# A hybrid decoder step on one core: the first four projection jobs taken on the centred input, the norm applied to their results

## The chip, the cores and the metric

The kernel runs on one core of one Trainium2 chip. The metric is the device time of one execution in microseconds. TensorE (PE, with its weight loads PEld) does matrix products and transposes, VectorE (DVE), ScalarE (ACT) and GpSimd (POOL) work element by element, SyncE (SP) issues most transfers. "Granted clock" is the share of the full TensorE clock that the profile shows as granted.

## The reference

One layer of a decoder with two head groups is applied to 272 prompt tokens (16 learned meta tokens and 256 of the prompt) and 32 sample tokens (8 x 4), 304 in all, width 2048. It starts with a LayerNorm, and what follows reads only its output:

```python
xp = _layernorm(concatenate([meta, x_prompt], axis=1), ln0_g, ln0_b)
xs = _layernorm(x_sample, ln0_g, ln0_b)
# in the layer
proj = x @ w_in                       # 2048 -> 7168
q, zf, v, g, gate_b, gate_c, xin = split(proj, ...)
zf = zf + b_f
...
mix = concatenate([o_a, y_b], axis=-1) @ w_o
h   = _layernorm(ALPHA * x + mix, ln1_g, ln1_b)
ff  = (silu(h @ w_gate) * (h @ w_up)) @ w_down
out = _layernorm(ALPHA * h + ff, ln2_g, ln2_b)
```

`_layernorm` is (x - mean) * rsqrt(var + eps) * gain + bias, per token. From q, zf, v and g a gated recurrence over the tokens is made for 8 heads (the scan), from the last three a gated convolution. All weights are float32 and are read once.

## The kernel before

**Projections as jobs.** Activations lie transposed in SBUF: channels on the partitions in 16 blocks of 128, tokens (304, or the 288 without meta tokens) along the free axis. Each weight matrix is read in pieces of 4 channel blocks by 256 columns, 512 KB. A piece is loaded by SP's queue into one of five raw buffers (`load_ahead`, L112; it runs five pieces ahead) and split in two (`split_next`, L128): "hi" is ScalarE's copy in the format fp32r, "lo" is VectorE's difference raw - hi. Up to five pieces lie split. The input is split in the same way into xh and xl. `run_job` (L169) makes 256 output columns: for each of 16 channel blocks and each of two PSUM banks, three products hi·xh, hi·xl and lo·xh (L184 to L186), 96 products a job. The first four jobs belong to the first pair of heads: zb (the forget gate), vb, qb and gb; then follow the other pairs, the convolutions, the output projection and the feed-forward part.

**What sets the order.** The instructions are put in order ahead of the run by a scheduler. It may move an instruction past others on its engine, except those that go through an `InOrder` wrapper (`vec`, `act`, `pe`), which stay in the order of the program; those show up under the wrapper's line, L56 (its shift through the change is to L58). The opening is written through these wrappers, the splits of the first eight pieces among them. TensorE, with 98% of the span, takes its instructions strictly in the order that results. Beside the jobs run "lanes" of small steps (`side`, `tick`, L146 to L161): after each channel block of a job every lane may do its next step. The lane "evac" copies the results of a job from PSUM after `LAG` = 4 ticks (`evac`), the lane "scan" does the recurrence.

**The opening** (L320 to L462). SP loads the meta tokens, the first half of the first 112 prompt rows, the short third token tile, the other halves, the second tile in two halves, then gain and bias of the first norm as 32 rows (`prow0`) and the weights. POOL makes the identity matrix and loads the other small parameters (`prows`, `crows`, `brow`). Tiles xt0 and xt1 hold 128 tokens each, xt2 the last 48. VectorE gets mean and variance of xt0 and xt1 with `bn_stats` on quarters, ScalarE the sums and squares of xt2; `rstd` (L350) makes 1/sqrt and refines it by one Newton step. `norm_rows` (L371) normalises the tiles in place, a quarter at a time, on VectorE and ScalarE. TensorE then transposes each block k (`turn`, L382, three transposes into one bank), and `settle` (L391) applies gain and bias (VectorE, tile xf), copies to xh (ScalarE) and subtracts for xl (every fourth on VectorE, the others on POOL). `turn` and `settle` run `LEAD` = 4 blocks ahead of the first job, zb, which is run inside the opening (L451). After it POOL makes the masks and constants for the scan (`make_constants`), TensorE transposes the parameter rows (L454 to L461), and `lower_bounds` (L275) works out the floor of the forget gate, for which ScalarE loads another function table (L273). The first piece is split block by block, its low part on POOL (L136).

## Time and profile before

| | |
|---|---|
| median of 3 runs | 1411.84 us (1411.36 to 1413.54) |
| profiled execution | 1411.89 us |
| its span | 1410.2 us |
| mean granted clock | 0.995 |
| busy PE | 1382.0 us, 98% |
| busy DVE | 831.2 us, 59% |
| busy ACT | 587.9 us, 42% |
| busy POOL | 115.6 us, 8% |
| moved by DMA | 231.12 MB, mean 164 GB/s |

The span counts from the first to the last event of the profiled execution; the rest of its time, 1.7 us, lies around it. The busy share is a mean over the whole kernel. The change touches the first part alone, so the stretches of the opening and the waits inside it say more than the shares. In rows of the timeline the first number is the start in us, the second the length; in square brackets stands how long the engine had been idle and what it waited for. In rows of groups "x16" is the count, then come total, mean (or least, median, greatest) times.

### The profile page before, as it was taken

The page shows a single profiled execution, that of the slowest core. Times are in us where ns is not written, and L with a number is a line of the kernel's source. Part 1 is how long each engine was busy: PE and PEld are TensorE (multiplying, and loading weights), DVE is VectorE, ACT ScalarE, POOL GpSimd, SP SyncE. Part 2 cuts the span into 40 slices and gives each one's busy share as a digit, 9 for nine tenths or more (in the row PEclk, how much of TensorE's full clock was granted, in tenths as well). Part 3 has the DMA queues.
Part 4 walks back from the last instruction along what each step waited for, and adds up shares of the span by engine and source line. Part 5 has one row for each costly group of instructions (what it writes and reads, how often), then busy time and mean ns, then how long its engine had stood idle before and what let it go on. Part 6 is the DMA issues. An engine that isn't in the chain of part 4 may idle for free.

```text
span 1410.2 us, 24922 instructions
## 1 busy us (share of the span) xinstructions
PE 1382.0 (98%) x10311; PEld 1365.6 (97%) x10311; DVE 831.2 (59%) x1342; ACT 587.9 (42%) x823; POOL 115.6 (8%) x174
## 2 busy tenths in 40 slices
PE   5999999999999999999999999999999999999996
PEld 4999999999999999999999999999999999999995
DVE  6756676876676888966444444444444444465444
ACT  5645544555443444434333333333333333343330
POOL 5201121111000332000000000000000000020000
PEclk9999999999999999999999999999999999999998
DMA  6655655555545554555555555555555555565541
GB/s 188 208 162 162 181 167 168 173 150 169 170 148 165 161 161 151 177 165 165 165 165 165 167 152 167 166 167 181 165 165 165 165 165 165 165 196 165 157 128 68
DMA packets 223858, 231.12 MB, mean 164 GB/s; under 512 B 7756, under 2 KB 219576, under 8 KB 223546
## 3 DMA queue, kind: packets, MB, share of 16 engines
q1 hardware_dynamic: 220240, 218.54, 50.9%
q0 software_dynamic: 3312, 10.72, 2.7%
q8 instruction: 81, 1.33, 0.4%
q10 hardware_dynamic: 192, 0.26, 0.1%
q14 instruction: 33, 0.27, 0.1%
HBM read 222.34 MB, written 7.15 MB: 163 GB/s over the span
## 4 chain that ended last, share of the span: by engine, by line
PE 98%; DVE 1%; POOL 1%; issue 0%; DVEq 0%; ACT 0%; POOLq 0%
PE u L184 7%; PE g L184 7%; PE wd L186 7%; PE g L185 7%; PE u L185 7%; PE wd L185 7%; PE g L186 7%; PE u L186 7%; PE wd L184 7%; PE wo L186 2%; PE wo L185 2%; PE wo L184 2%; PE zb L184 2%; PE zb L185 1%; PE zb L186 1%; PE vb L184 1%
## 5 line engine op out<-in xcount | busy, mean ns | idle before, releaser
L75 DVE TENSOR_TENSOR lo<-raw,hi 128x1024 fp32r<-128x1024 f32 (+1 forms) x408 | 501.7, 1231 | 476.5 <-ACT hi L74 476.0
L74 ACT CAST hi<-raw 128x1024 fp32r<-128x1024 f32 (+1 forms) x408 | 421.3, 1033 | 635.5 <-PE u L185 162.6
L185 PE MATMUL wd<-al,hi 128*128 128x288 f32 x704 | 207.9, 295 | 0.0
L184 PE MATMUL wd<-ah,hi 128*128 128x288 f32 x704 | 207.8, 295 | 0.0
L186 PE MATMUL wd<-ah,lo 128*128 128x288 f32 x704 | 207.8, 295 | 0.0
L184 PE MATMUL g<-ygh,hi 128*128 128x288 f32 (+1 forms) x452 | 134.0, 296 | 0.0
L185 PE MATMUL u<-ygl,hi 128*128 128x288 f32 (+1 forms) x452 | 133.9, 296 | 0.0
L185 PE MATMUL g<-ygl,hi 128*128 128x288 f32 (+1 forms) x452 | 133.9, 296 | 0.0
L184 PE MATMUL u<-ygh,hi 128*128 128x288 f32 (+1 forms) x452 | 133.8, 296 | 0.0
L186 PE MATMUL g<-ygh,lo 128*128 128x288 f32 (+1 forms) x452 | 133.6, 296 | 0.0
L186 PE MATMUL u<-ygh,lo 128*128 128x288 f32 (+1 forms) x452 | 133.6, 296 | 0.0
L185 PEld LDWEIGHTS wd<-al,hi 128*128 128x128 f32 x704 | 132.3, 188 | 0.0
L186 PEld LDWEIGHTS wd<-ah,lo 128*128 128x128 f32 x704 | 132.2, 188 | 0.0
L184 PEld LDWEIGHTS wd<-ah,hi 128*128 128x128 f32 x704 | 132.1, 188 | 0.1
L186 PEld LDWEIGHTS u<-ygh,lo 128*128 128x128 f32 x452 | 85.4, 189 | 0.0
L184 PEld LDWEIGHTS g<-ygh,hi 128*128 128x128 f32 x452 | 85.3, 189 | 0.1
L186 PEld LDWEIGHTS g<-ygh,lo 128*128 128x128 f32 x452 | 85.3, 189 | 0.0
L185 PEld LDWEIGHTS g<-ygl,hi 128*128 128x128 f32 x452 | 85.3, 189 | 0.1
L185 PEld LDWEIGHTS u<-ygl,hi 128*128 128x128 f32 x452 | 85.3, 189 | 0.0
L184 PEld LDWEIGHTS u<-ygh,hi 128*128 128x128 f32 x452 | 85.3, 189 | 0.0
L186 PE MATMUL wo<-mh,lo 128*128 128x288 f32 x256 | 75.9, 296 | 0.0
L185 PE MATMUL wo<-ml,hi 128*128 128x288 f32 x256 | 75.6, 295 | 0.0
(391 smaller groups left out, 3132.3 us busy)
## 6 DMA issues: line engine op xcount, KB each, us to landing
raw<-in_w_in SPq DMA_DIRECT2D x112, 512.0 KB, 3.7
raw<-in_w_gate SPq DMA_DIRECT2D x88, 512.0 KB, 3.6
raw<-in_w_up SPq DMA_DIRECT2D x88, 512.0 KB, 3.6
raw<-in_w_down SPq DMA_DIRECT2D x79, 512.0 KB, 3.6
raw<-in_w_o SPq DMA_DIRECT2D x32, 512.0 KB, 3.6
s<-in_state_hgrn POOLq DMA_DIRECT2D x8, 512.0 KB, 5.5
out<-sn POOLq DMA_DIRECT2D x8, 512.0 KB, 4.4
raw<-in_w_down SPq DMA_DIRECT2D x15, 256.0 KB, 2.8
```

Source lines behind the costliest of these rows:

```text
L74: a.copy(out=hi, in_=src)
L75: v.tensor_tensor(out=lo, in0=src, in1=hi.bitcast(F32), op=ALU.subtract)
L184: nc.tensor.matmul(o, hi[:, i % kb, cs], xh, start=(i == 0), stop=False)
L185: nc.tensor.matmul(o, hi[:, i % kb, cs], xl, start=False, stop=False)
L186: nc.tensor.matmul(o, lo[:, i % kb, cs], xh, start=False, stop=(i == nk - 1))
```

## The change

The first four jobs no longer read the normalised input. They read the tokens with gain applied and roughly centred, and the norm is applied to their results. This is possible because the norm only scales and shifts each token: with c any number per token, x_norm·W = r·[(x - c)·g·W] + r·(c - mean)·[g·W] + [b·W]. The last two brackets are columns that don't depend on the token.

- c (`xcen`) is the token's mean over the first channel block alone, made by one product with a matrix of 1/128 (`ones_h`). `settle` subtracts it in VectorE from the transposed block (xc), ScalarE multiplies with the gain (mh), VectorE makes the low part in one step (ml). The gain g and the bias b stand as two more columns behind the tokens in mh and ml, so that products of these jobs are 306 or 290 wide and yield g·W and b·W.
- Mean and variance are got during the first job: `bn_stats` on quarters after the first two blocks of each four, the sums of xt2 (`row_sums`) on ScalarE at blocks 13 and 15. Behind the job's last product, `rstd` gives r and -mean·r per token, two groups of three products (rb) spread them over the partitions, and xr = r and xnm = c·r - mean·r are made.
- `evac_raw` takes the place of `evac` for the first four jobs: copy of the two columns, multiply by xr, add xnm times the first column, and then the job's own step with the second column as bias.
- The real xh and xl, which later jobs need, are made in a new lane "norm" (`normed_input`) during jobs two to four, 48 steps. After the fourth job `open_scan` ends that lane, gives the memory to the scan, and calls `make_constants`, which stood behind the first job.
- Loads: the tokens come in quarters of 512 channels. ScalarE's queue takes the first quarter of the three short pieces, SP the quarters of xt0 and xt1 with whole weight pieces between. POOL's queue takes the rows of gain and bias (they were SP's last before the weights), then the rest of the short pieces and the other rows.
- The low part of the first piece goes from POOL to VectorE, `LEAD` from 4 to 3, and two products (`WARM`) without use for the result open TensorE's work. sfin has one buffer instead of two.

The core of the diff:

```diff
-LEAD = 4
+LEAD = 3
+NXC = 4
+WARM = 2
...
-                nc.gpsimd.tensor_tensor(out=lo[:, k], in0=raw[:, k], in1=hi[:, k].bitcast(F32), op=ALU.subtract)
+                vec.tensor_tensor(out=lo[:, k], in0=raw[:, k], in1=hi[:, k].bitcast(F32), op=ALU.subtract)
...
+        for dst, src in small:
+            act.dma_start(out=dst[:, :XC], in_=src[:, :XC])
+        tc.keep_in_program_order(nc.scalar.preload_act_table_set("sqrt_and_others"))
+        for c in range(NXC):
+            cs = slice(c * XC, (c + 1) * XC)
+            nc.sync.dma_start(out=xts[0][NMETA:, cs], in_=xin[: P - NMETA, cs])
+            nc.sync.dma_start(out=xts[1][:, cs], in_=xin[P - NMETA : 2 * P - NMETA, cs])
+            load_to(c + 1)
         load_ahead(0)
+        pool.memset(ones_h, 1.0 / P)
+        load_rows(pool, prow0, 0, ("ln0_g", "ln0_b"))
+        for dst, src in small:
+            pool.dma_start(out=dst[:, XC:], in_=src[:, XC:])
...
+        for _ in range(WARM):
+            nc.tensor.matmul(warm, ident, ident.unsqueeze(1).broadcast_to([P, 4, P]), start=True, stop=True)
...
         def settle(k):
             if k < NB:
-                b = xT.pop(k)
-                xf = x0w.tile([P, T], F32, tag="xf", name="xf", bufs=4)
-                vec.tensor_scalar(out=xf, in0=b[:, :T], scalar1=pcol("ln0_g", k), scalar2=pcol("ln0_b", k), op0=ALU.mult, op1=ALU.add)
-                act.copy(out=xh[:, k], in_=xf)
-                xfs[k] = xf
+                vec.tensor_tensor(out=xc[:, k], in0=xT.pop(k)[:, :T], in1=xcen, op=ALU.subtract)
+                act.activation(out=mixh[:, k, :T], in_=xc[:, k], func=AF.Copy, scale=pcol("ln0_g", k))
             if k:
-                eng = vec if k % 4 == 1 else nc.gpsimd
-                eng.tensor_tensor(out=xl[:, k - 1], in0=xfs.pop(k - 1), in1=xh[:, k - 1].bitcast(F32), op=ALU.subtract)
+                vec.scalar_tensor_tensor(out=mixl[:, k - 1, :T], in0=xc[:, k - 1], scalar=pcol("ln0_g", k - 1),
+                                         in1=mixh[:, k - 1, :T].bitcast(F32), op0=ALU.mult, op1=ALU.subtract)
...
+        turn(0)
+        x0c = x0p.tile([P, T], F32, name="x0c")
+        vec.tensor_copy(out=x0c, in_=xT[0][:, :T])
         pb = bank("pb", "main")
-        nc.tensor.transpose(pb[:, :NP0], prow0, ident[:NP0, :NP0])
+        nc.tensor.transpose(pb[:, T : T + NP0], prow0, ident[:NP0, :NP0])
+        nc.tensor.matmul(pb[:, :T], ones_h, x0c, start=True, stop=True)
+        act.copy(out=xcen, in_=pb[:, :T])
...
         def first_rhs(k):
-            c = k // 2 + 2
-            if k % 2 == 0 and c < 4:
-                norm_rows(0, c, act)
-                norm_rows(1, c, vec)
-                norm_rows(2, c, vec)
             if k + LEAD < NB:
-                turn(k + LEAD, (0, 1, 2))
+                turn(k + LEAD)
             if k + LEAD <= NB:
                 settle(k + LEAD)
-            return xh[:, k], xl[:, k]
-
-        first_job = run_job(first_rhs, T, "zb")
-        make_constants()
+            c, i = divmod(k, 4)
+            if i < 2:
+                vec.bn_stats(out=bns[i][:, c], in_=xts[i][:, c * XC : (c + 1) * XC])
+            if k in (13, 15):
+                next(sums)
+            return mixh[:, k], mixl[:, k]
+
+        first_job = run_job(first_rhs, T + 2, "zb")
+        for i in range(2):
+            vec.bn_aggr(out=sts[i][0], in_=bns[i])
+        for _ in zip_longest(*(rstd(i) for i in range(3))):
+            pass
+        rb = [bank("rb") for _ in range(2)]
+        for q in range(2):
+            for i in range(3):
+                nc.tensor.matmul(rb[q][:, i * P : i * P + rows[i]], rn[:, i, q : q + 1].broadcast_to([P, P]), ident[:, : rows[i]],
+                                 start=True, stop=True)
+        act.copy(out=xr, in_=rb[0][:, :T])
+        vec.tensor_mul(out=xnm, in0=xcen, in1=xr)
+        vec.tensor_tensor(out=xnm, in0=xnm, in1=rb[1][:, :T], op=ALU.add)
...
+    def evac_raw(n, banks, out, tag, fn):
+        yield LAG
+        for j in range(2):
+            t = ep_.tile([P, n], F32, tag=tag, name=tag, bufs=4)
+            u = ep_.tile([P, 2], F32, tag="u", name="u", bufs=2)
+            nc.vector.tensor_copy(out=u, in_=banks[j][:, n : n + 2])
+            nc.vector.tensor_mul(out=t, in0=banks[j][:, :n], in1=xr[:, T - n :])
+            nc.vector.scalar_tensor_tensor(out=t, in0=xnm[:, T - n :], scalar=u[:, 0:1], in1=t, op0=ALU.mult, op1=ALU.add)
+            fn(j, t, t, u[:, 1:2])
```

In the orders below a row holds line, operation, output<-inputs and the output's shape; numbers behind names tell tiles apart.

The start of TensorE's order, before: the rows of gain and bias are transposed first (pb from prow0), then four blocks of xt0, of xt1 and of xt2.

```order
L423 MATMUL pb_193<-ident_72,prow0_67 128x32
L387 MATMUL xT_208<-ident_72,xt0_103 128x128
L387 MATMUL xT_210<-ident_72,xt0_103 128x128
L387 MATMUL xT_212<-ident_72,xt0_103 128x128
L387 MATMUL xT_214<-ident_72,xt0_103 128x128
L387 MATMUL xT_208<-ident_72,xt1_104 128x128
```

The same place now: L397 is `turn`, L426 the transpose of those rows, L427 the product that gives c.

```order
L369 MATMUL warm_156<-ident_69 128x512 x2
L397 MATMUL xT_170<-ident_69,xt0_109 128x128
L397 MATMUL xT_170<-ident_69,xt1_110 128x128
L397 MATMUL xT_170<-ident_69,xt2_111 128x128
L426 MATMUL pb_176<-ident_69,prow0_106 128x32
L397 MATMUL xT_181<-ident_69,xt0_109 128x128
L397 MATMUL xT_181<-ident_69,xt1_110 128x128
L397 MATMUL xT_181<-ident_69,xt2_111 128x128
L397 MATMUL xT_185<-ident_69,xt0_109 128x128
L397 MATMUL xT_185<-ident_69,xt1_110 128x128
L397 MATMUL xT_185<-ident_69,xt2_111 128x128
L427 MATMUL pb_176<-x0c_174,ones_h_79 128x304
```

The transpose of prow0 has moved behind the first block, and the product for c stands behind it and six further transposes.

VectorE's order inside the first job, before: gain and bias (xf), low parts (xl, every fourth), tokens normalised in place, and the low part of a weight piece (lo).

```order
L56 TENSOR_SCALAR xf_254<-xT_250,pvec_69 128x304
L56 TENSOR_SCALAR xf_268<-xT_264,pvec_69 128x304
L56 TENSOR_TENSOR xl_96<-xf_254,xh_95 128x304
L56 TENSOR_SCALAR xt1_104<-xt1_104,mv1_142,r1_144 128x512
L56 TENSOR_SCALAR xt2_105<-xt2_105,mv2_147,r2_149 48x512
L56 TENSOR_SCALAR xf_285<-xT_281,pvec_69 128x304
L56 TENSOR_SCALAR xf_299<-xT_295,pvec_69 128x304
L56 TENSOR_TENSOR lo_312<-raw_120,hi_311 128x1024
```

And now, about the same blocks: xnm still holds c here, and each subtraction (xc) is followed by a low part (ml).

```order
L58 TENSOR_TENSOR xc_102<-xT_229,xnm_93 128x304
L58 SCALAR_TENSOR_TENSOR ml_98<-xc_102,pvec_67,mh_97 128x304
L58 BN_STATS bn1_160<-xt1_110 128x6
L58 TENSOR_TENSOR xc_102<-xT_243,xnm_93 128x304
L58 SCALAR_TENSOR_TENSOR ml_98<-xc_102,pvec_67,mh_97 128x304
L58 TENSOR_TENSOR xc_102<-xT_256,xnm_93 128x304
L58 SCALAR_TENSOR_TENSOR ml_98<-xc_102,pvec_67,mh_97 128x304
L58 TENSOR_TENSOR lo_272<-raw_126,hi_271 128x1024
```

Every block now has a low part on VectorE, the statistics stand between them, and the low part of a weight piece stands directly behind that of a block.

ScalarE's order at the end of the first job, before: the last two xh, two weight casts, the function table and the exponentials of `lower_bounds` (ee, lse), and an activation of the scan (w1).

```order
L56 CAST xh_95<-xf_409 128x304
L56 CAST xh_95<-xf_423 128x304
L56 CAST hi_435<-raw_124 128x1024
L56 CAST hi_439<-raw_309 128x1024
L273 ACT_TABLE_LOAD
L285 ACTIVATE ee_523<-dd_520 128x16
L507 ACTIVATE w1_998<-z_605 128x304
L289 ACTIVATE lse_527<-es_525 128x8
L56 CAST hi_561<-raw_371 128x1024
L56 CAST hi_565<-raw_433 128x1024
```

And now: the sums of xt2 (junk, s2), three square roots (t0 to t2), the copy of r (xr), the table and the exponentials.

```order
L58 ACTIVATE mh_97<-xc_102,pvec_67 128x304
L58 ACTIVATE junk_415,s2_416<-xt2_111 48x2048
L58 ACTIVATE junk_415,s2_416<-xt2_111,s2_416 48x2048
L58 ACTIVATE t0_163<-mv0_161,epsb_146 128x1
L58 ACTIVATE t1_166<-mv1_164,epsb_146 128x1
L58 ACTIVATE t2_169<-mv2_167,epsb_146 48x1
L58 COPY xr_92<-rb_463 128x304
L274 ACT_TABLE_LOAD
L286 ACTIVATE ee_485<-dd_482 128x16
L290 ACTIVATE lse_489<-es_487 128x8
L58 CAST hi_512<-raw_329 128x1024
L58 CAST hi_516<-raw_389 128x1024
```

The two casts of the second job's last pieces (hi_512 and hi_516 here) still stand behind the table and the exponentials, but the chain of the statistics is now ahead of those.

More of the change, by code (lines that the diff above doesn't have):

```diff
@@ L112, in load_ahead, with load_to @@
     def load_ahead(i):
[L113 removed]
+        load_to(i + AHEAD_DMA)
+    def load_to(n):
+        while state["dma"] < min(len(pieces), n):
             p = state["dma"]
@@ L380, in hybrid_step, with turn @@
-        xT = {}
-        def turn(k, tiles):
-            if k not in xT:
-                xT[k] = bank("xT")
-            for i in tiles:
-                n = rows[i]
-                nc.tensor.transpose(xT[k][:, i * P : i * P + n], xts[i][:n, k * P : (k + 1) * P], ident[:n, :n])
-        xfs = {}
+        xT = {}
+        def turn(k):
+            xT[k] = bank("xT")
+            for i in range(3):
+                nc.tensor.transpose(xT[k][:, i * P : (i + 1) * P], xts[i][:, k * P : (k + 1) * P], ident)
@@ new lines, in hybrid_step @@
+        turn(0)
+        x0c = x0p.tile([P, T], F32, name="x0c")
+        vec.tensor_copy(out=x0c, in_=xT[0][:, :T])
+        pb = bank("pb", "main")
+        nc.tensor.transpose(pb[:, T : T + NP0], prow0, ident[:NP0, :NP0])
+        nc.tensor.matmul(pb[:, :T], ones_h, x0c, start=True, stop=True)
+        act.copy(out=xcen, in_=pb[:, :T])
+        vec.tensor_copy(out=pvec[:, :NP0], in_=pb[:, T : T + NP0])
+        for k in range(1, LEAD):
+            turn(k)
+        for k in range(LEAD):
+            settle(k)
```

197 lines of the change are left out of this document (97 added, 100 removed).

## The prediction

> **What bounds the kernel now.** Time per stage comes first, then TensorE's waits, then its timeline through the opening. Columns of the first fence: stretch in us, its length, busy time with instruction count of PE, PEld, DVE, ACT, POOL, granted clock, DMA share, GB/s.
>
> ```profile
> 0.00:20.00 20.00, 3.57 (x14) 2.29 (x14) 9.72 (x36) 9.93 (x16) 12.24 (x53) 1.00 0.92 262
> 20.00:40.80 20.80, 20.77 (x109) 17.03 (x108) 16.30 (x26) 11.30 (x21) 9.95 (x13) 1.00 0.32 96
> 58.74:84.00 25.26, 25.26 (x194) 25.26 (x193) 14.91 (x25) 12.05 (x19) 3.55 (x1) 1.00 0.59 180
> ```
>
> TensorE does nearly nothing for 20 us and is then always busy. So a change in the opening is worth exactly what it moves a fixed point of TensorE's order; I take the first product of the third job (qb), behind which nothing on TensorE changes but two columns. The waits (total, times, longest, in us) and the timeline (start, length) say where it stands:
>
> ```profile
> PE pb L423 <- DMA prow<-in_ln_b: 13.2, 1, 13.2
> PE mb L56 <- DVE mq L56: 2.3, 1, 2.3
> PE xT L387 <- DVE xt L56: 1.9, 1, 1.9
> ...
> PE ca L962 <- DVE yc L1012: 0.4, 1, 0.4
> ...
> 20.15 0.85 PE L184 MATMUL zb<-xh,hi 128*128 128x304 f32 x2
> 24.11 0.46 PE L184 MATMUL zb<-xh,hi 128*128 128x304 f32 x1
> 24.36 0.46 PE L185 MATMUL zb<-xl,hi 128*128 128x304 f32 x1
> 28.58 0.30 PE L186 MATMUL zb<-xh,lo 128*128 128x304 f32 x1
> 28.72 0.30 PE L184 MATMUL zb<-xh,hi 128*128 128x304 f32 x1
> 58.74 0.29 PE L184 MATMUL qb<-xh,hi 128*128 128x288 f32 x1
> ```
>
> The first product starts at 20.15; until about 28.1 products step by 0.25 us, later by 0.14 (the clock rows show 1.00 throughout). qb starts at 58.74. The profiled run took 1411.89 us, its span 1410.2; the median of the runs is 1411.84, so no correction lies between them. A measurement can tell about 0.2%, 2.8 us: "same" is 1409.1 to 1414.7.
>
> **The change: the start.** The norm's chain before the first product goes. In its place TensorE's order has the ln0 rows' transpose ahead of six token transposes and of the mean's product, so all of them wait for two row transfers, which the change moves from SP to POOL's queue. Prices:
>
> ```profile
> 2.12 0.32 POOL masks.py:199 TENSOR_SCALAR_AFFINE_SELECT ident<-ident 128x128 f32<-128x128 f32 x1
> 2.36 0.54 POOL L211 DMA_DIRECT2D prows<-in_lb_param  x1
> ...
> prows<-in_lb_param POOLq DMA_DIRECT2D x1, 8.0 KB, 5.8
> prows<-in_gnorm_g POOLq DMA_DIRECT2D x1, 4.0 KB, 6.8
> ...
> out<-sfin POOLq DMA_DIRECT2D x8, 64.0 KB, 3.5
> ...
> 14.48 1.12 PE L387 MATMUL xT<-ident,xt 128*128 128x128 f32 x4 [0.95 <-ACT xt L56]
> 123.16 0.65 PE L666 MATMUL nb<-w,ones_h 128*128 128x288 f32 x2
> 17.33 0.17 DVE L56 COPY pvec<-pb 128x32 f32<-128x32 f32 x1
> L749 ACT COPY vT<-vb 128x304 f32<-128x304 f32 x2 | 0.8, 416 | 0.4 <-PE vb L186 0.4
> ```
>
> The second row transfer follows the identity's select and one memset, so it is issued at about 2.5. Such transfers land 5.8 to 6.8 us later when the queues are full, 3.5 when they are not: 6.0 to 9.3, and I take 8.3, since 2.5 MB lies in SP's queue then as now. Then 0.28 for the transpose, 1.5 for six more, 1.2 for the mean's product (0.65 at full step, up to double at the slow one), 0.42 and 0.17 for the two copies: VectorE subtracts the first block's mean at 11.9. The second token quarter sits behind four weight pieces in SP's order, 3.1 MB; the transfers of before had moved that much at 13.4, and the first product can't start before 14.8 (casts and gain columns, 2.9 us): no cost.
>
> ```profile
> GB/s 0 145 308 173 180 292 382 262 349 348 348 349 342 20 15 285 50 57 293 0 0 5 43 317 1 0 193 156 0 55 145 324 352 281 339 350 350 344 348 338
> ```
>
> (Slices of 1.5 us.)
>
> **The change: the first job.** VectorE now has, until it subtracts block 15: 16 subtractions from PSUM, 14 low halves, 6 row statistics, 4 quarter pieces and 5 whole pieces of weights. Rows of the same forms:
>
> ```profile
> 97.68 0.98 DVE L746 TENSOR_SCALAR z<-zb,pvec 128x304 f32<-128x304 f32 x2 [0.72 <-PE zb L186]
> L830 DVE SCALAR_TENSOR_TENSOR ygl<-yc,pvec,ygh x16: 505/1058/1068, 466.6 to 548.2; 128x288 fp32r<-128x288 f32 x16
> 12.68 2.47 DVE L56 BATCH_NORM_STATS2 bn<-xt 128x6 f32<-128x512 f32 x4
> 60.29 0.42 DVE L556 TENSOR_TENSOR w<-b 128x256 f32<-128x256 f32 x1
> 60.63 1.22 DVE L75 TENSOR_TENSOR lo<-raw,hi 128x1024 fp32r<-128x1024 f32 x1
> 61.76 0.18 DVE L557 TENSOR_TENSOR w<-b 128x32 f32<-128x32 f32 x1
> 31.61 1.32 DVE L56 TENSOR_TENSOR lo<-raw,hi 128x1024 fp32r<-128x1024 f32 x1 [1.46 <-ACT hi L56]
> L829 ACT ACTIVATE ygh<-yc,pvec x16: 520/536/541, 466.0 to 546.0; 128x288 fp32r<-128x288 f32 x16
> L56 ACT CAST hi<-raw 128x1024 fp32r<-128x1024 f32 x7 | 7.1, 1041 | 0.0
> ```
>
> From start to start (an instruction begins about 0.08 before its forerunner's printed end): 16 x 0.45 = 7.2, 14 x 0.45 = 6.3 (the fast end of 505 to 1058: the slow ones stand beside POOL's sums, and POOL has none here), 6 x 0.61 = 3.7, 4 x 0.34 = 1.4, 5 x 1.13 = 5.7, in all 24.3. To that come waits. Three of the whole pieces stand directly behind a low half, while ScalarE's cast of that piece stands behind the gain product of the newest block: 0.54 + 1.04 after that block's subtraction, of which the low half covers 0.45. That is about 1.2 us each, 3.6 (0 to 1.46 each: the row at 31.61 is such a wait). The first blocks wait 1.0 for ScalarE. So block 15 is subtracted 28.9 after the start, at 40.8. Each four blocks take 7.1 us. TensorE alone would need from 14.8: 96 + 18 products at 0.14, 30 transposes at 0.2 and 3.2 us for the slow clock, to 39.7; VectorE is the later by some 3 us, and the 18 products of the second job that stand early in its order are hidden in that.
>
> **The change: behind the first job.** TensorE has the second job's first two pieces, then the two broadcasts of the norm (rb), the parameter transposes, then pieces 6 and 7, whose casts on ScalarE stand behind the statistics, xr's copy, the table load and the lower bounds.
>
> ```profile
> 8.03 1.91 ACT L56 ACTIVATE junk<-xt 48x2048 f32<-48x2048 f32 x1 [5.94 <-DMA xt<-in_x_sample]
> 10.14 0.13 DVE L56 TENSOR_SCALAR mv<-s 48x1 f32<-48x1 f32 x1
> 15.06 0.13 DVE L56 TENSOR_SCALAR mv<-s 48x1 f32<-48x1 f32 x1
> 16.50 0.26 DVE L56 TENSOR_TENSOR r<-r,t 128x1 f32<-128x1 f32 x2
> ...
> L273 ACT ACT_TABLE_LOAD x5 | 6.4, 1283 | 0.1
> ...
> 41.62 0.66 PE L461 MATMUL bufT<-ident,brow 16*128 16x16 f32 x8
> 44.39 0.22 ACT L285 ACTIVATE ee<-dd 128x16 f32<-128x16 f32 x1
> ```
>
> Counted from block 15's subtraction: gain product 0.5, sum pass 2.1 (8.03 to 10.14), its small steps 0.25, square pass 2.1: 5.0. From the variance to r two chains took 1.7, three get 1.9: 6.9. TensorE is out of products at about 6.5 and waits. rb 0.7: 7.6; copy 0.4: 8.0; table load 1.3: 9.3. Beside it the second rb and the transposes (0.6 + 0.5 + 0.66) end at 9.4, their copies and differences at 10.0, the lower bounds' three small steps at 10.8. Cast of piece 6: 11.8; its low half, behind the first evacuation steps, 13.4; then the 44 products left of the second job at 0.14: 19.5. TensorE idles for two stretches of about 2.4 us. qb starts at 11.9 + 28.9 + 19.5 = 60.3, 1.6 later than 58.74.
>
> **The change: jobs three and four.** Two columns more in 384 products are 384 x 0.9 ns, half of it before qb and hidden: 0.2. VectorE has per job 4 pieces (4.5), 16 norm steps at 0.39 (6.2) and the evacuation (2.0), 12.7 against TensorE's 12.6 (25.26 for two), with pieces about 3 us ahead at qb: hidden, if nothing slips. The constants now follow the fourth job on POOL; the scan needs them a job later. sfin's single buffer is free 3.5 us after its issue, heads apart.
>
> Sum: 1411.9 + 1.6 + 0.2 = 1413.7.
>
> **The rivals.** (1) The early start is kept: rows land after 3.5 us (at 6.0) and the casts aren't waited for: 2.3 + 3.6 less, 1407.8. For it: the queues hold fewer long token packets; against it: the order and the row at 31.61. (2) Slower, by the clock: TensorE's two gaps of 2.4 us around the lower bounds, with 0.6 us of products between, bring the 0.25 step back for as long as it lasted at the start, 8.0 us (20.15 to 28.1). That loses 8.0 x (1 - 0.14/0.25) = 3.5: 1417.2. It decides from the gap at which the step falls back; once the step is fast, before has no wait over 0.4 (that for yc) up to the 2.3 (mq) in the chain that closes the kernel, so nothing here excludes it. [...] No run here shows it yet. (3) Jobs three and four: if each of their eight pieces loses 0.75 us to ScalarE's queue, 6 us against a reserve of 3: 1416.7. (4) That the quarters don't help, since SP issues four pieces ahead of the second, is in the sum.
>
> **How the numbers follow.** Forecast 0.48, with a range of its own of 1411 to 1416.5 (rows landing 1 us either way, waits of 0.8 to 1.46, a subtraction at 0.42 to 0.49); rivals 0.22, 0.17, 0.13. Faster: most of (1), 0.19. Same: two thirds of the forecast and the rest of (1), 0.42. Slower: the forecast's upper third, (2) and (3), 0.39. The range reaches to (1) and past (2): 1408 to 1418.
>
> **What would show it.** Right: the first token subtraction at 11 to 13, four blocks in 7 us with a wait of over 1 us ahead of each whole piece, TensorE idle for 4 to 6 us between the second job's halves behind ACT, qb at 59 to 62. Wrong: products without gaps after the first job, or rows landed by 6; a 0.25 step after 50 would show (2); TensorE waiting for lo after 62 (3).

## The result, and the profile after

| | before | after |
|---|---|---|
| median of 4 runs | 1412.22 us (1411.36 to 1413.54) | 1424.82 us (1423.44 to 1426.71) |
| profiled execution | 1411.89 us | 1426.71 us |
| its span | 1410.2 us | 1425.0 us |
| busy PE, DVE, ACT | 1382.0, 831.2, 587.9 us | 1394.4, 860.4, 604.2 us |

The change makes the kernel slower: ratio 1.0089, 95% interval 1.0072 to 1.0107, or 12.6 us between the medians. The profiled execution after is the longest of its four; it is 14.8 above that of before. The forecast was 1413.7, with a range to 1418.

TensorE's fixed points show where that comes from. The rows are those of its timeline after, at the places that the prediction used, and at two later ones: the first head's key transposes (ktb) and the first product of its output norm (nb, at 123.16 before).

```profile
9.29 0.22 PE L426 MATMUL pb<-ident,prow 32*128 32x32 f32 x1 [1.50 <-DMA prow<-in_ln_b]
18.92 0.45 PE L397 MATMUL xT<-ident,xt 128*128 128x128 f32 x1 [6.57 <-DMA xt<-in_x_prompt]
21.25 0.60 PE L189 MATMUL zb<-mh,hi 128*128 128x306 f32 x1
55.79 0.62 PE L189 MATMUL vb<-mh,hi 128*128 128x306 f32 x1 [2.36 <-ACT hi L58]
58.12 0.46 PE L190 MATMUL vb<-ml,hi 128*128 128x306 f32 x1
58.38 0.46 PE L191 MATMUL vb<-mh,lo 128*128 128x306 f32 x1
65.19 0.30 PE L189 MATMUL qb<-mh,hi 128*128 128x290 f32 x1
120.81 0.44 PE L626 MATMUL ktb<-ident,kp 128*128 128x128 f32 x2 [2.15 <-DVE kp L595]
135.88 0.65 PE L696 MATMUL nb<-w,ones_h 128*128 128x288 f32 x2
```

The first product of zb is 1.1 late (21.25 against 20.15), qb 6.45 (65.19 against 58.74), nb 12.7, and the end 14.8. So the delay grows in three stretches: by 5.3 between the first product and qb, by 6.3 between qb and nb, and by 2.1 behind nb. Four losses make it up, each with a wait or a rate of its own; the first of them begins ahead of zb's first product.

**First, the second token quarter.** The window view of the first 20 us has 210 GB/s in its last column, where before had 262:

```profile
0.00:20.00 20.00, 8.37 (x20) 4.03 (x20) 10.88 (x20) 6.07 (x12) 12.81 (x45) 0.74 0.96 210
```

VectorE's timeline holds the first subtraction (12.30, with the one after it), that of block 4, and that of block 15:

```profile
12.30 0.84 DVE L58 TENSOR_TENSOR xc<-xT,xnm 128x304 f32<-128x304 f32 x2
23.38 0.47 DVE L58 TENSOR_TENSOR xc<-xT,xnm 128x304 f32<-128x304 f32 x1 [3.28 <-PE xT L397]
27.66 1.22 DVE L58 TENSOR_TENSOR lo<-raw,hi 128x1024 fp32r<-128x1024 f32 x1 [1.12 <-ACT hi L58]
43.60 0.47 DVE L58 TENSOR_TENSOR xc<-xT,xnm 128x304 f32<-128x304 f32 x1
```

The quarter that holds blocks 4 to 7 lands at 18.9. TensorE waits 6.57 for it, VectorE 3.28 behind that.

**Second, the clock.** Stretches of the window view after: two ahead of a fall of the granted clock, and the two behind them. The first number behind the stretch is its length, the second TensorE's busy time; the clock is the third from the right. The stretches are cut where the clock changes, or 3.41 us ahead of that.

```profile
50.74:54.15 3.41, 2.37 (x22) 2.18 (x22) 2.16 (x17) 1.72 (x3) 0.00 (x0) 1.00 0.02 5
54.15:60.98 6.83, 5.17 (x19) 4.80 (x20) 6.83 (x17) 6.00 (x9) 0.00 (x0) 0.50 0.36 109
119.01:122.42 3.41, 1.61 (x13) 1.44 (x14) 3.41 (x11) 2.99 (x8) 0.00 (x0) 1.00 0.31 97
122.42:129.25 6.83, 6.83 (x34) 5.71 (x33) 4.15 (x11) 0.53 (x3) 1.41 (x2) 0.50 0.64 185
```

Behind the opening the clock falls to a half twice, for 6.8 us each time. The first time it falls at 54.15, inside the wait for the casts; the 18 products between 55.79 and 60.93 then take 5.1 instead of 2.5. Of the difference 2.1 are the half clock's (0.255 from start to start instead of 0.141), 0.5 lie in two longer steps, at 55.79 and 56.72. The second time it falls at 122.42, behind the wait of 2.15 for kp; half of the 6.83, 3.4 us, is an estimate of the work lost in it.

**Third, VectorE.** The stretch from 60 to 110 us in the kernel before and in the one after, and the first step of the first head's scan in each (w<-z on ScalarE):

```profile
60.00:110.00 50.00, 50.00 (x377) 49.37 (x376) 28.29 (x45) 22.96 (x35) 4.48 (x2) 1.00 0.54 159
45.77 0.46 ACT L507 ACTIVATE w<-z 128x304 f32<-128x304 f32 x1 [1.16 <-DVE z L746]
```

```profile
60.00:110.00 50.00, 49.92 (x363) 49.68 (x362) 45.52 (x95) 40.30 (x64) 2.98 (x10) 0.99 0.64 191
98.95 0.46 ACT L537 ACTIVATE w<-z 128x304 f32<-128x304 f32 x1
```

VectorE (the third pair of numbers) goes from 28 to 45.5 us of 50, and the scan of the first head, which before ran beside jobs two to four, begins 53 us later.

**Fourth, a rate.** The dense jobs of the feed-forward part, 670 to 800 us, before and after:

```profile
670.00:800.00 130.00, 130.00 (x981) 130.00 (x980) 58.23 (x61) 49.22 (x61) 0.00 (x0) 1.00 0.54 166
```

```profile
670.00:800.00 130.00, 130.00 (x976) 130.00 (x975) 58.12 (x61) 49.29 (x61) 0.00 (x0) 1.00 0.54 166
```

Nothing in this stage was edited, TensorE is busy throughout at the full clock, and yet five products fewer fit into 130 us: 0.1332 instead of 0.1325 each (between the starts of the rows themselves, 0.1334 and 0.1328 in the mean, the figures of the expectations below).

### The profile page after: what moved, and what is told of

It reads as the page before. It is cut to its first block, busy times and chain, and to the rows that moved or that the text cites. A ratio compares the mean times of both kernels' runs of the same rounds, so it can differ in the third digit from the quotient of the medians.

```text
span 1425.0 us, 25072 instructions
## 1 busy us (share of the span) xinstructions
PE 1394.4 (98%) x10329; PEld 1374.9 (96%) x10329; DVE 860.4 (60%) x1432; ACT 604.2 (42%) x854; POOL 104.6 (7%) x164
## 4 chain that ended last, share of the span: by engine, by line
PE 94%; DVE 2%; ACT 2%; DMA 1%; issue 1%; SPq 0%; DVEq 0%; ACTq 0%
PE u L190 7%; PE g L190 7%; PE g L189 7%; PE u L189 7%; PE wd L191 7%; PE wd L190 7%; PE u L191 7%; PE g L191 7%; PE wd L189 7%; PE wo L191 2%; PE wo L190 2%; PE wo L189 2%; PE xb L189 1%; PE qb L189 1%; PE cb L189 1%; PE qb L190 1%
## 5 line engine op out<-in xcount | busy, mean ns | idle before, releaser
L191 PE MATMUL g<-ygh,lo 128*128 128x288 f32 (+1 forms) x452 | 133.6, 296 | 0.0
L191 PE MATMUL u<-ygh,lo 128*128 128x288 f32 (+1 forms) x452 | 133.6, 296 | 0.0
L189 PEld LDWEIGHTS wd<-ah,hi 128*128 128x128 f32 x704 | 132.3, 188 | 0.1
```

Of the source, the lines that this page charges most:

```text
L189: nc.tensor.matmul(o, hi[:, i % kb, cs], xh, start=(i == 0), stop=False)
L191: nc.tensor.matmul(o, lo[:, i % kb, cs], xh, start=False, stop=(i == nk - 1))
```

## The experiments

Theory at the start: the four losses are independent, and each has the cause just named. The rival for the first two is that the wait only moves. Each time is the median of 4 to 10 runs (of one run for e13 and e14); the kernel before had medians of 1411.97 to 1413.01 beside them.

**e1: weight pieces between the token quarters.** `load_to(n)` tests `state["dma"] < min(len(pieces), n)`, and inside its loop unpacks a piece into `w, k0, n, c0, mc`. That sets n to 4, the piece's length, so the first call issues four pieces and not one.

```diff
-    def load_to(n):
-        while state["dma"] < min(len(pieces), n):
+    def load_to(last):
+        while state["dma"] < min(len(pieces), last):
```

> The loop that loads weight pieces up to a given number reuses the name of its bound for the piece's length, so that it issues four pieces at its first call; here only that name is changed, and SP's order becomes a token quarter, one piece, the next quarter, one piece, and so on. Theory A (the late second quarter costs): the second quarter lands by about 10 us instead of 18.9, the 3.3 us wait of VectorE ahead of the subtraction of block 4 goes, everything behind it is 3.3 us earlier, while the wait for the casts behind the first job, the slow clock there and the wait for kp stay: 1424.8 - 3.3 = 1421.5. Rival (the weights were needed as early): the second and third pieces are late instead, and the time stays at 1424.8 within 1.

Measured: 1421.43 (1420.68 to 1421.74), 3.4 less. TensorE and VectorE in this run, and two window stretches about its wait for kp:

```profile
16.25 0.62 PE L189 MATMUL zb<-mh,hi 128*128 128x306 f32 x1 [0.31 <-ACT hi L58]
63.11 0.30 PE L189 MATMUL qb<-mh,hi 128*128 128x290 f32 x1
118.73 0.44 PE L626 MATMUL ktb<-ident,kp 128*128 128x128 f32 x2 [2.15 <-DVE kp L595]
```

```profile
20.67 0.46 DVE L58 TENSOR_TENSOR xc<-xT,xnm 128x304 f32<-128x304 f32 x1
```

```profile
114.24:117.66 3.42, 2.34 (x17) 2.10 (x16) 3.42 (x7) 2.23 (x6) 1.48 (x1) 1.00 0.70 237
117.66:121.07 3.41, 2.34 (x21) 2.10 (x25) 3.29 (x11) 2.83 (x8) 0.00 (x0) 1.00 0.49 153
```

Block 4 is subtracted at 20.67 without a wait, 2.7 earlier, and qb comes 2.1 earlier. The first 20 us have 215 GB/s, hardly more than the 210 after, so it is the order of the transfers that gives this back and not their rate.

The wait for kp is the same 2.15, but this time the clock stays at 1.00. In the trace of after the moments at which the clock changes lie whole multiples of 3.413 us apart (6.37, 9.78, 23.43, 54.15, 60.98, 122.42 and 129.25; from the first to the last it is 36 times 3.413). In e1 the slow step of 0.255 ends at 59.6, and 17 times 3.413 behind that is 117.66. On that grid e1's wait (116.58 to 118.73) is cut at 117.66 into two halves, as the two stretches above show, while 1.8 of the 2.15 us after lie in the one stretch that ends at 122.42. From qb to nb TensorE takes 70.7 us after and 67.6 in e1, e3 and e5, which wait 2.13 to 2.35 at ktb and keep the clock. So the same gap costs 2.1 here and 3.1 more in the other execution. What differs between the two is how the gap lies on the grid; two executions show no more than that.

**e2: casts early.** The splits of pieces 6 and 7 go ahead of the two sums of the third token tile.

```diff
             if k in (13, 15):
+                split_next()
                 next(sums)
```

> Pieces 6 and 7 are split ahead of the sums of the third token tile, instead of behind the chain of the statistics. Theory (TensorE runs out of products behind the first job, and the gap brings the half clock): TensorE has 48 more products during the chain, the waits of 0.5 and 2.4 us and most of the half clock's 2.3 us go, the chain itself is 1 to 2 us later; qb starts near 60.5 instead of 65.2: 1420.1. Rival (qb is held by the evacuation of zb, which needs the norm): the wait moves ahead of qb and the time falls by less than 2: above 1422.8.

Measured: 1419.25 (1417.72 to 1420.02), 5.6 less.

```profile
60.30 0.37 PE L189 MATMUL qb<-mh,hi 128*128 128x290 f32 x1
113.90 0.44 PE L627 MATMUL ktb<-ident,kp 128*128 128x128 f32 x2 [1.76 <-DVE kp L596]
```

```profile
35.31:38.73 3.42, 1.85 (x12) 1.23 (x10) 3.42 (x7) 1.01 (x2) 0.00 (x0) 1.00 0.31 84
38.73:42.14 3.41, 3.41 (x13) 3.41 (x14) 2.30 (x6) 2.27 (x5) 0.00 (x0) 0.50 0.20 69
```

qb starts at 60.30; there is no wait between the halves of vb, and no half clock there. The evacuation of zb did not hold qb. The clock does fall once in this execution, inside the first job at 38.73, where TensorE waits for VectorE's blocks; so does it in e4, at 36.62.

**e3: the gap filled.** The gap behind the first job is left as it is, and products without use run in it.

```diff
+        fill = bank("fill")
+        for _ in range(3):
+            pe.matmul(fill, ident, ident.unsqueeze(1).broadcast_to([P, 4, P]), start=True, stop=True)
         bb_ = bank("bufT")
```

> Three more products of the identity with itself (512 columns, no use for the result) stand behind the transposes of the parameter rows, in the gap ahead of pieces 6 and 7; nothing else changes. Clock theory (an idle stretch halves TensorE's clock for a fixed time): the wait for the casts ends at the same time, but the granted clock stays at 1.00 and the products behind it step by 0.14 at once instead of 0.25 for 5.1 us: qb 2.3 earlier, less 0.2 for the last filler, 1422.7. Rival (the slow step comes from the casts or from VectorE): steps stay at 0.25 and the time at 1424.8 or 0.3 above.

Measured: 1423.44 (1420.78 to 1424.66), 1.4 less, within the scatter. Its rows say more than its time:

```profile
50.70 2.84 PE L58 MATMUL fill<-ident 128*128 128x512 f32 x6
54.52 0.31 PE L190 MATMUL vb<-ml,hi 128*128 128x306 f32 x1
55.96 0.62 PE L191 MATMUL vb<-mh,lo 128*128 128x306 f32 x2 [0.85 <-DVE lo L58]
56.38 0.46 PE L189 MATMUL vb<-mh,hi 128*128 128x306 f32 x1
```

The four products behind the fillers run at the full step, 0.14, as the clock theory has it. Then a wait of 0.85 for the low half follows on the transposes of bufT and the short burst, and the clock falls after all, at 56.30, for 3.4 instead of 6.8 us; the rows from 56.38 on step by 0.255. In these rows the step follows the clock, not the casts; that the fillers would keep the clock for good was wrong. The time itself decides nothing here: with the same order of loads, zb's first product lay anywhere from 19.02 (e3) to 22.13 (e5), as the second token quarter landed.

**e4: scan memory early.** The scan's first tiles get a memory pool of their own behind the first job (gate chain, keys, values, first states); `make_constants` goes there too.

```diff
-    sp = reset = kdm = vtm = at_b = nbuf = None
+    sp = kdm = at_b = nbuf = None
+    se = s2.enter_context(tc.tile_pool(name="se", bufs=1))
+    reset, vtm = (se.tile([P, n], F32, name=name) for name, n in (("reset", T), ("vtm", P)))
+    make_constants()
...
-            return sp.tile([P, n], dt, tag=tag, name=tag, **kw)
+            return se.tile([P, n], dt, tag=tag, name=tag, **kw)
```

> The scan's first tiles (gate chain, keys, values, the first states) and its constants get memory of their own behind the first job, instead of waiting until the centred input is given back after the fourth; only the tiles of its later steps still wait. Theory (the change pushed the first head's scan from jobs two to four to behind them, so that TensorE waits 2.15 us for kp and gets the half clock for 6.8 us): the first head's activations start near 62 instead of 99, no wait at ktb, clock 1.00 there: 1424.8 - 5.5 = 1419.3. Rival (VectorE and ScalarE are full in jobs two to four with the norm of the input, so the scan gains nothing): a wait at ktb or for a weight piece's low half stays, above 1422.8.

Measured: 1422.46 (1421.41 to 1425.0), 2.4 less. In the profiled execution zb starts 2.0 earlier (19.29) and ktb's wait brings no half clock, so the 2.4 can't be put down to the edit. The scan begins at 61.87, and kp is late all the same:

```profile
60.00:110.00 50.00, 50.00 (x367) 49.98 (x366) 47.70 (x97) 39.73 (x66) 2.13 (x4) 0.99 0.59 179
61.87 0.45 ACT L539 ACTIVATE w<-z 128x304 f32<-128x304 f32 x1
112.32 0.44 PE L628 MATMUL ktb<-ident,kp 128*128 128x128 f32 x2 [1.88 <-DVE kp L597]
```

VectorE is full with it. The theory that the late begin makes the wait falls; the rival, VectorE's load, stands.

**e5, e6, e13, e14: the rate in the feed-forward part.** The change moves five tiles out of the constants' memory, 3776 bytes per partition, and all that lies behind starts lower: the weight buffers hi begin at byte 41824 instead of 45600, while nmh, which holds 7 of the 16 channel blocks that these jobs read (the other nine lie in ygh), stays at 147296. An unused tile among the constants displaces the weight buffers: in the changed kernel by 128 bytes, in the kernel before by 320, 832 and 160.

```diff
+    pad = const.tile([P, 32], F32, name="pad")
+    nc.gpsimd.memset(pad[:, 0:1], 0.0)
```

> An unused tile of 128 bytes per partition stands among the constants, so that the weight buffers (raw, hi, lo) and what lies behind them start 128 bytes further on; no instruction changes but one small memset. In every kernel with the change, each product of the jobs that read nmh takes 0.13341 us from start to start, before 0.13277, some 3300 products or 2.1 us in all. Address theory (the change takes 3776 bytes out of the constants' memory, and hi then starts at the same place modulo 1024 bytes as nmh): with hi 128 bytes on, the step is 0.1328 again and the time falls by 2.1 to 1422.7. Rival (the step belongs to what else the change does, or only to the old place): the step stays at 0.1334 and the time at 1424.8, within 1.

> The kernel before, with an unused tile of 320 bytes per partition among its constants, which puts hi at the same place modulo 1024 bytes as nmh, as in the changed kernel; nothing else changes. Address theory: the step of the jobs that read nmh rises from 0.1328 to 0.1334, and the time by 2.1, to 1414.3. Rival: step and time as in the kernel before, 1412.2 within 0.7.

> The kernel before with an unused tile of 832 bytes per partition among the constants: hi at 352 modulo 1024, nmh at 864; they agree modulo 512 but not modulo 1024. If agreement modulo 512 is enough, the step of the jobs that read nmh is 0.1334, as with both at 864; if it must be modulo 1024, 0.1328.

> The kernel before with an unused tile of 160 bytes: hi at 704 modulo 1024, nmh at 864, no agreement modulo 512 either. If agreement is the condition, the step is 0.1328; if every displacement but the old one and that of 128 bytes in the changed kernel costs, 0.1334.

The stretch of 670 to 800 us in e5, e6, e13 and e14, in this order:

```profile
670.00:800.00 130.00, 130.00 (x983) 130.00 (x982) 57.77 (x62) 50.11 (x63) 0.00 (x0) 1.00 0.54 166
```

```profile
670.00:800.00 130.00, 130.00 (x977) 130.00 (x976) 57.78 (x61) 49.52 (x61) 0.00 (x0) 1.00 0.54 166
```

```profile
670.00:800.00 130.00, 130.00 (x977) 130.00 (x976) 57.18 (x61) 49.42 (x61) 0.00 (x0) 1.00 0.53 163
```

```profile
670.00:800.00 130.00, 130.00 (x981) 130.00 (x980) 57.66 (x61) 49.48 (x61) 0.00 (x0) 1.00 0.54 166
```

| kernel | hi modulo 512 | nmh modulo 512 | products in 130 us | time |
|---|---|---|---|---|
| before | 32 | 352 | 981 | 1412.2 |
| after | 352 | 352 | 976 | 1424.8 |
| e5: after, +128 | 480 | 352 | 983 | 1420.76 (1419.36 to 1423.52) |
| e6: before, +320 | 352 | 352 | 977 | 1414.49 (1413.06 to 1416.27) |
| e13: before, +832 | 352 | 352 | 977 | 1415.11, one run |
| e14: before, +160 | 192 | 352 | 981 | 1412.94, one run |

In the three of these kernels where the weight buffers and nmh agree modulo 512 bytes, 976 or 977 products fit; in the three where they do not, 981 to 983. The kernel before becomes slower by a memset of one column and 320 unused bytes, ratio 1.0013 (1.0004 to 1.0023). In e13 they agree modulo 512 and not modulo 1024, and 977 fit as in e6. But nmh lies at 352 in all six, so these runs don't tell agreement with nmh from the weight buffers' place 352 itself. Nor is it the products of nmh alone that slow down: between 670 and 802 us those of ygl with hi start 135.0 ns behind the product before them after and in e13, 132.9 before and 132.3 in e14, those of nmh with lo 133.5 and 133.6 against 132.1 and 132.6. e5 fell by more than 2.1 (4.1). No half clock came with its wait for kp in the profiled execution, which fits, but its four runs lie 4 us apart, so the rest is not explained.

**e7: loads and casts mended.** e1, e2 and the 128 bytes of e5 in one kernel.

> The name of the loop's bound is mended, so that one weight piece goes between two token quarters, pieces 6 and 7 are split ahead of the sums of the third token tile, and the tile of 128 bytes is in. If the three losses add (late quarter 3.4, gap and half clock behind the first job 5.6, address 2.1): 1424.8 - 11.1 = 1413.7; qb starts near 57.5. If the evacuation of zb holds qb, or the earlier start only makes a longer wait for the chain of the norm: above 1416. The wait for kp of about 2 us is left.

Measured: 1412.91 (1411.52 to 1416.15), ratio to before 1.0007 (0.9997 to 1.0017). The losses add as the theory said: 11.9 of 11.1 expected.

```profile
55.47 0.37 PE L189 MATMUL qb<-mh,hi 128*128 128x290 f32 x1
109.04 0.44 PE L630 MATMUL ktb<-ident,kp 128*128 128x128 f32 x2 [1.76 <-DVE kp L599]
```

```profile
60.00:110.00 50.00, 47.66 (x348) 46.81 (x346) 50.00 (x105) 40.36 (x68) 6.18 (x11) 1.00 0.63 190
```

qb now comes 3.3 earlier than in the kernel before, and nb at 123.49, no earlier: between the two the early start is given back. VectorE is busy for all 50 us. The clock does not fall once in this execution between 17.8 and the end of the work.

**e8: norm on POOL, and early memory.** e7 with e4's memory, and the two tensor steps of `normed_input` on POOL.

```diff
-            nc.vector.tensor_mul(out=x, in0=x, in1=xr)
+            nc.gpsimd.tensor_mul(out=x, in0=x, in1=xr)
             yield 1
-            nc.vector.tensor_add(out=x, in0=x, in1=xnm)
+            nc.gpsimd.tensor_add(out=x, in0=x, in1=xnm)
```

> As the run with loads and casts mended, and in addition the norm of the input in jobs two to four is multiplied and added on the idle POOL instead of VectorE (32 steps of 0.47 there), and the scan's first tiles have memory of their own. Theory (the wait at ktb comes from the late start of the first head's scan and from VectorE's load): no wait for kp, 2.1 and what of the half clock still stands there less, 1411.5 or lower. Rival (POOL's steps slow VectorE through contention, or the norm becomes late): a wait of over 1 us stays in jobs three to six, 1413 to 1416.

Measured: 1430.27 (1430.15 to 1430.79), 17 more than e7. It is worse by far than the rival had it.

```profile
PE ktb L632 <- DVE kp L601: 8.2, 1, 8.2
PE qb L189 <- DVE z L783: 7.4, 1, 7.4
...
L503 POOL TENSOR_TENSOR xc<-xc,xr x16: 822/876/1820, 53.2 to 83.2; 128x304 f32<-128x304 f32 x16
L505 POOL TENSOR_TENSOR xc<-xc,xnm x16: 822/1064/1818, 58.8 to 85.0; 128x304 f32<-128x304 f32 x16
```

```profile
L77 DVE TENSOR_TENSOR xl<-xc,xh 128x304 fp32r<-128x304 f32 x16 | 11.5, 734 | 0.0
```

A step that takes VectorE 0.47 takes POOL 1.03 in the mean, and beside it VectorE's own subtraction of the same size takes 0.73 instead of 0.47. VectorE is relieved of 15 us and slowed in the rest, and zb's evacuation makes TensorE wait 7.4. The scan began at 94.5 here in spite of its own memory, so this run says nothing of an early begin.

**e9: without the norm's steps.** e7, with the three steps taken out of `normed_input`. The kernel leaves the norm out of what the later jobs read, so its results differ and only its time is of use.

> As the run with loads and casts mended, but without the multiplication, the addition and the gain and bias of the norm of the input in jobs two to four (later jobs read the centred input instead of the normalised one; the splits stay): 32 steps of 0.47 us less on VectorE, 16 of 0.64 less on ScalarE. Theory (VectorE is full from 60 to 110 us, and this makes kp late): the wait for kp goes, and the other delays between qb and nb with it: 1412.9 - 3 = 1410. Rival (the scan begins late because of its memory): the wait for kp stays near 1.8, 1412.9.

Measured: 1410.02 (1409.48 to 1410.98), ratio to before 0.9979 (0.9969 to 0.9989).

```profile
60.00:110.00 50.00, 50.00 (x375) 49.37 (x375) 37.46 (x75) 28.13 (x44) 6.24 (x12) 1.00 0.64 190
99.62 0.38 PE L626 MATMUL ktb<-ident,kp 128*128 128x128 f32 x2
```

VectorE has a quarter of the stretch free, ktb waits for nothing, and nb comes at 121.54, 1.6 ahead of the kernel before. This is what the early start is worth when nothing is full behind it: some 2 to 3 us. Two other things change with it: ScalarE's load falls from 40 to 28 us, and the scan begins at 66.05 instead of 92.59.

**e10: the scan held back in the kernel before.** The other half of the test: a late scan with VectorE not full.

```diff
         z, vT, q, sg = zs[j], vs[j], qs[j], gs[j]
+        if h < 2:
+            nc.vector.scalar_tensor_tensor(out=z[:, :L], in0=sg, scalar=0.0, in1=z[:, :L], op0=ALU.mult, op1=ALU.add)
```

> The kernel before, with the first head pair's z held back until their gate sg is ready (z plus zero times sg, two steps of 0.5 us on VectorE), so that the scan begins after the fourth job as it does with the change, while VectorE is not full. Theory of VectorE's load: the chain has time enough, the wait at ktb is under 0.5, time 1412.8 within 0.7. Rival (a late scan is enough): a wait of about 2 us at ktb, 1414.8 or more.

Measured: 1414.03 (1412.31 to 1414.62), ratio 1.0005 (0.9995 to 1.0014): no difference.

```profile
60.00:110.00 50.00, 49.77 (x373) 48.66 (x372) 29.82 (x53) 27.39 (x44) 2.33 (x1) 1.00 0.53 161
103.63 0.44 PE L598 MATMUL ktb<-ident,kp 128*128 128x128 f32 x2
```

The scan begins at 91.33 and kp is still in time. Early and full (e4) waits 1.9, late and free (e10) does not wait: it is the load and not the late begin. ScalarE's load goes along with VectorE's in these runs (27 us here, 40 in e4 and e7), and none separates the two; what speaks for VectorE is that it had no idle time at all in e7, while ScalarE had a fifth of the stretch free.

**e11: key transposes later; e12: no warm-up.** Both are e7 with one edit.

```diff
-        yield 3
+        yield 3 if h else 15
...
-            nc.tensor.transpose(ktb[:, c * P : (c + 1) * P], kp[:, c, 1:3].rearrange("p a b -> p (a b)"), ident)
+            (nc.tensor if h else pe).transpose(ktb[:, c * P : (c + 1) * P], kp[:, c, 1:3].rearrange("p a b -> p (a b)"), ident)
```

> As the run with loads and casts mended, with the first head's key transposes pinned 17 products (2.3 us) later in TensorE's order; nothing is taken from VectorE. If the wait for kp of 1.8 us is what is lost there: no wait at ktb and 1412.9 - 1.8 = 1411.1. Rival (the scan behind it becomes late by as much, since VectorE's queue is the limit): a wait of similar size at a later step, 1412.9.

> As the run with loads and casts mended, without the two products that open TensorE's work. If they bring the full clock earlier: the first products step by 0.25 for longer than in that run (there till 17.7), a loss of up to 1.5, 1414.4; if the transposes and the first products do it alone: the same within 0.5. A gain is not expected by either.

e11: 1411.79 (1411.21 to 1412.63), 1.1 under e7, ratio to before 0.9991 (0.9981 to 1.0000). It is the shortest of the complete kernels, by an amount at the edge of what the runs can tell. Of the wait for kp, 0.9 is left in the waits view. e12: 1412.18 (1411.32 to 1415.89), not distinguishable from e7: the two opening products do nothing for the time that these runs can tell.

**e15, e16: early memory once more.** e15 is e7 with e4's memory, e16 has e11's edit as well.

> As the run with loads and casts mended, with the scan's first tiles in memory of their own, so that the scan may begin early while VectorE keeps the norm's steps. If VectorE's load alone decides: the wait for kp of about 1.8 stays, 1412.9 within 0.7. If the early begin gives the chain a share of its time back: up to 1.5 less, 1411.4.

> As e15, and the first head's key transposes pinned later in TensorE's order. VectorE's load: as the run with these transposes later alone, 1411.8 within 0.7. With a share for the early begin: no wait for kp at all, 1410.9.

e15: 1412.55 (1411.82 to 1413.06), the wait at ktb is 1.60. e16: 1412.09 (1411.34 to 1412.62). An early begin changes the time by 0.4 less (e15 against e7) and 0.3 more (e16 against e11), both within the scatter.

## Why the prediction was wrong

The forecast (1413.7) put the loss behind the first job in the right place, but four of its terms were missing or too small, and all four on one side.

- **"Rows land at 8.3, VectorE subtracts at 11.9."** Right, in part by luck: the row transfers were there at 9.29 (range 6.0 to 9.3), 1.0 late, and the steps behind them took 3.0 instead of 3.6, so that the first subtraction came at 12.30.
- **"The second token quarter ... no cost."** This step failed. I took the moment by which the transfers of before had moved 3.1 MB, 13.4. After the change the quarter landed at 18.9, and e1 gives 2.1 (at qb) to 3.4 (in the time) back. I had read from the order that four pieces stand ahead of the quarter, and took the rate of before and a strict order. By the window views after, 3.1 MB had moved at 15.4 (200 GB/s), 2.0 later than before; by 18.9 it was 4.0 MB, so 0.9 MB of other transfers had gone through as well.
- **"Four blocks in 7.1 us, waits of 1.2 for the casts."** Right: from block 7 to block 11 VectorE took 6.8 (28.80 to 35.63), with waits of 1.1. Block 15 came at 43.6 instead of 40.8: the 3.28 of the quarter and the 0.4 of the start, less 0.9.
- **"19.5 from there to qb."** This step failed by the half clock, which the sum put at nothing. It took 21.6: products went on 12.2 behind block 15 instead of 13.4, but 48 of them stood there and not 44 (0.6), the half clock added 2.1 and the two longer steps 0.5. Rival (2) had this mechanism with a chance of 0.17. Its price was 3.5; the falls cost 2.1 at the casts and 3.1 at ktb. Its place was right once; the second place was not seen. I gave it so little because I took the two waits of 2.4 us to be too short for it. No run shows that the half clock costs nothing there, as the sum had it: the gap behind the first job, 2.36 of it the wait for the casts, brought it in the kernel after and in e1, e4 and e5. In the kernel after, a wait of 2.15 at ktb with 1.61 us of work in the stretch of 3.41 brought it too. The changes of the clock in its trace lie on a grid of 3.413 us, and the same wait of 2.15 cost the half clock in one execution and not in another (e1).
- **"Jobs three and four ... hidden, if nothing slips."** This step failed, by omission. I counted 12.7 us of VectorE per job against TensorE's 12.6, but only pieces, norm steps and evacuation. The kernel before already had the first head's scan in that time (w<-z at 45.77); it had to go somewhere, and VectorE was full until 110. The wait for kp and the smaller delays between qb and nb cost 2.9 (e7 against e9), and 3.1 more where the half clock came with it. That "the scan needs them a job later" was said of the constants, and taken as no cost for the chain.
- **No step at all** stood for the 2.1 us in the feed-forward part. The change removes five tiles from the constants' memory, and I did not ask what their addresses decide. e6 makes that loss, 1.7 against the kernel before, with no other edit.
- **Rival (1), the early start kept,** was not tested as it stood. With the losses mended and the norm's steps left out (e9) the kernel is 3.0 under the one before, where the rival had 4.1 (1407.8), but not by the rival's way: the rows were there at 8.7 and not at 6.0.
- **Rival (3)** named VectorE's saturation, for weight pieces; its victim was the scan's kp.
- **Two slips in the working.** TensorE's own sum to the end of the first job gives 40.0, not 39.7. By the parts named, the chances are 0.35 for "same" and 0.46 for "slower", not 0.42 and 0.39. Neither changes the forecast.

The sum then is: 1412.2, less some 2.5 for the early start, 3.4 for the quarter, 5.6 for the gap with its half clock, 2.9 for VectorE's load and 2.1 for the addresses, 1423.7. The 1.1 left to 1424.8 are less than what the half clock at ktb adds in some executions. The terms come from different runs with a scatter of 1 to 2 us each, so the sum shows that the losses are of the right size and no more.

## What to carry to other kernels

Work that is moved off the start goes into a stage that has work of its own: count all that runs there already, the side lanes too, before calling it hidden. When a change moves tiles between memory pools, compare the start-to-start time of a stage that was not edited (here 0.1332 against 0.1325). A gap in TensorE's work can have two prices, itself and the half clock behind it: here 2.15 for the wait at ktb, and 3.1 more after but not in e1, with the gap lying differently on the grid of 3.413 us.

## What the runs showed of the hardware

- The clock changed at moments that are whole multiples of 3.413 us apart: after, at the seven moments given under e1; in e8 at 34.57, 37.98, 61.87, 68.70, 113.07 and 123.31; in e9 at 8.04, 11.45, 14.87 and 18.28. A half clock behind the start lasted 3.4 us (e2, e3, e4, e8), 6.8 (after, e1, e4, e5, e8) or 10.2 (e8, behind a wait of 8.2 for kp).
- How much idle time brings it, these runs don't settle. It followed on stretches of 3.41 us in which TensorE was busy for 1.61 (ktb after), 1.85 (e2 at 38.73), 2.37 (after at 54.15) and 2.42 (e3 at 56.30). It did not follow on 1.65 (e7, with the whole wait of 1.76 in one stretch, if the grid is counted on from 17.8, where the fast step begins), nor on two stretches of 2.34 (e1). The stretches of 2.37 and 2.42 held the broadcast products or fillers and the small transposes; no run tells which kind of work counts.
- Products of 288 columns took 0.1331 to 0.1332 (670 to 800 us) where the weight buffers lay at 352 modulo 512 bytes, as nmh does, and 0.1322 to 0.1325 where they lay at 32, 192 or 480. Which pair of tiles is at fault stays open, since all weight buffers and the hidden tiles move together. Agreement of a product's own two operands was not enough in the wd jobs: hi and the hidden tile ah agree modulo 512 in both kernels, and 755 and 756 products fit into 100 us before and after, 0.1324.

```profile
850.00:950.00 100.00, 100.00 (x755) 100.00 (x755) 42.95 (x47) 34.28 (x35) 0.00 (x0) 1.00 0.53 163
```

```profile
850.00:950.00 100.00, 100.00 (x756) 100.00 (x755) 43.52 (x47) 33.14 (x35) 0.00 (x0) 1.00 0.54 165
```

- The granted clock reads 1.00 in the opening until its first event, though products step by 0.25 there (20 to 28 us before, 14.85 to 17.8 in e7): there the step is the surer sign.
- With two tensor steps of 128 x 304 per block on POOL (e8), VectorE's step of that size took 0.73 in the mean instead of 0.47, and the low part of a weight piece 1.39 instead of 1.22.
